# Making the low parts of projection weights on VectorE, and summing the first block's modulation shifts on TensorE

## The chip, the cores and the metric

The kernel runs on one core of a Trainium2 chip. The metric is the device time of one execution in microseconds (us). A core has TensorE (PE in the profile: matmuls, with weight loads as PEld), VectorE (DVE), ScalarE (ACT), GpSimd (POOL) and SyncE (SP), whose queue here issues nearly all DMAs. Each engine works through a queue of its own, in an order that is fixed when the kernel is compiled; semaphores tie the queues together.

## The reference

One layer of a decoder trunk on 512 tokens of width 2048: a conditioned norm, a mixer of two head groups, and a retrieval feed-forward. What matters for the change is the beginning:

```
c_act = jax.nn.silu(c)                                  # one vector of 2048
mod = (c_act @ ada_w[l] + ada_b[l])[:, None, :]         # 2048 x (6*2048)
sh1, sc1, g1, sh2, sc2, g2 = jnp.split(mod, 6, axis=-1)
h = rmsnorm(x, mix_norm_g[l]) * (1.0 + sc1) + sh1
proj = h @ w_in                                         # 2048 x 3920
```

After that come norms of the latents, the up-projections, attention and gated linear attention, the output projection, a second conditioned norm and the feed-forward. The change touches none of these.

## The kernel before

**Products in three parts.** A float32 weight tile is loaded (`wraw`, L267), cast to a rounded high part by ScalarE (`whi`, L115), and the low part is the difference `wlo = wraw - whi` (L117). `split` has an argument that says which engine subtracts: VectorE by default, GpSimd where `load_w` is called with `"gpsimd"`. The activations have parts `hhi` and `hlo` (L303, L304). `mm3` (L107 to L110) then multiplies high by high (L108), high weight by low activation (L109), and low weight by high activation (L110): the low part of the weight is asked for by the third matmul.

**Start.** x arrives in four DMAs of 1 MB. Its squares are summed by VectorE and GpSimd (L163), TensorE sums them over partitions (L167), VectorE makes the reciprocal root (`rstd`, L145 to L151), TensorE spreads it (L156) and ScalarE copies it to `rr` (L206). GpSimd then multiplies the 16 tiles of x by `rr` (L209).

**Modulations.** `mod_acc` sums one section of `c_act @ ada_w` for a range of columns on VectorE: for each of the 16 tiles of 128 rows it loads a piece of `ada_w` (`adaw`, L222, six buffers), multiplies it by the tile's column of `cact` and adds it to `acc` (L226 for the first, L228 for the rest). `mod_col` then sums `acc` over the partitions with one matmul for each 128 columns (L238) and adds the bias (L240); for a scale it also applies the norm's gain (L244). Scales of the first norm go to `A1`, shifts to `B1`.

**First stage.** The 16 tiles of h are worked in five blocks, `KBLOCKS` = 3, 3, 3, 4 and 3 tiles. For each block, all scales and shifts of its columns must be there (`for _ in late`); then ScalarE makes `xT * A1` (L302) and `hhi` (L303), VectorE `hlo` (L304), and 15 tiles of weight columns are multiplied with the block: 9 matmuls each, or 12 in the block of four. From the second block on VectorE adds each result to the earlier ones (L316). While a block is multiplied, `advance(3)` after each weight tile issues the modulations of the next block; these are 32 pieces, 16 for scales and 16 for shifts. Before the first block nothing else is there for TensorE to do, so its 32 pieces stand ahead of all products.

**Second stage.** Eight more weight tiles (`gr`, L428) with all 16 tiles of h, and then the two halves of `w_gv` (L436), 16 pieces each. Beside these, VectorE sums the modulations for later stages, with 128 x 512 pieces, and works on the latents' norms, the rotary tables and the gates. Weights of both stages have five buffers for `wraw` and four each for `whi` and `wlo`; in both, the low parts are made by GpSimd. The up-projections after them have theirs made by VectorE already.

Of the kernel before, what the change touches and what calls it, by code (L numbers as in the profile page):

```python
# [16 lines left out]
OP = mybir.AluOpType  # L17
# [4 lines left out]
P = 128  # L22
T = 512
TB = 4
D = 2048
KD = 16
# [26 lines left out]
KBLOCKS = ((0, 3), (3, 3), (6, 3), (9, 4), (13, 3))  # L53
# [33 lines left out]
def hybrid_layer(ctx, tc, a, out):  # L87
    nc = tc.nc
# [12 lines left out]
    def bank(tag):  # L101
        return cur[tag][0].tile([P, 512], F32, name="b_" + tag, tag=tag)

    mm = nc.tensor.matmul
# [23 lines left out]
    vec = {}  # L128
# [3 lines left out]
    cact = const.tile([P, KD], F32, name="cact")  # L132
    nc.scalar.activation(cact, vec["c_t"], AF.Sigmoid)
    nc.vector.tensor_tensor(out=cact, in0=cact, in1=vec["c_t"], op=OP.mult)
    A1 = const.tile([P, KD], F32, name="A1")
    B1 = const.tile([P, KD], F32, name="B1")
# [52 lines left out]
    hhi, hlo = [[h0[n][:, k, :] if k < NLAT else h1[n][:, k - NLAT, :] for k in range(KD)] for n in range(2)]  # L189
    wp = pools.push("w", RIGHT, bufs=4)  # L190
# [21 lines left out]
    ada_v = a["ada_w"].rearrange("(k p) n -> p k n", p=P)  # L212

    def ada_tile(pool):
        return pool.tile([P, 512], F32, name="adaw", tag="adaw", bufs=NADA)
# [16 lines left out]
    def mod_col(pool, sec, dst, c0, width):  # L232
        for acc in mod_acc(pool, sec, c0, width):
            yield
        b = bank("m")
        n0, nn = c0 // P, width // P
        for n in range(nn):
            mm(b[:, n:n + 1], acc[:, n * P:(n + 1) * P], ones, start=True, stop=True)  # L238
        d = dst[:, n0:n0 + nn]
        nc.vector.tensor_tensor(out=d, in0=b[:, :nn], in1=vec["ada_b_t"][:, sec * KD + n0:sec * KD + n0 + nn],  # L240
                                op=OP.add)
        if sec in (1, 4):
            g = vec["mixg"] if sec == 1 else vec["ffng"]
            nc.vector.scalar_tensor_tensor(out=d, in0=d, scalar=1.0, in1=g[:, n0:n0 + nn], op0=OP.add, op1=OP.mult)  # L244

    def mod_both(pool, c0, width):
        for acc in mod_acc(pool, 5, c0, width):
            yield
        brow = ada_tile(pool)
        nc.sync.dma_start(out=brow[0:1, :], in_=a["ada_b"][:, 5 * D + c0:5 * D + c0 + width])  # L250
        yield
        b = bank("m")
        n0, nn = c0 // P, width // P
        for n in range(nn):
            mm(b[:, n:n + 1], acc[:, n * P:(n + 1) * P], ones, start=True, stop=True)
        nc.vector.tensor_tensor(out=G2[:, n0:n0 + nn], in0=b[:, :nn],
                                in1=vec["ada_b_t"][:, 5 * KD + n0:5 * KD + n0 + nn], op=OP.add)
        b = bank("m")
        mm(b[0:1, :], ones, acc, start=True, stop=False)
        mm(b[0:1, :], ones[0:1, :], brow[0:1, :], start=False, stop=True)  # L260
        nc.scalar.copy(out=acc[0:1, :], in_=b[0:1, :])
        nc.sync.dma_start(out=g2d[:, c0:c0 + width], in_=acc[0:1, :])


    def load_w(pool, src, shape, lo_eng="vector"):
        raw = pool.tile(shape, F32, name="wraw", tag="wraw", bufs=5 if pool is wp else NWRAW)
        nc.sync.dma_start(out=raw, in_=src)  # L267
        return split(pool, raw, shape, "whi", "wlo", lo_eng=lo_eng)
# [6 lines left out]
    def both(*gens):  # L275
        gens = list(gens)
        while gens:
            for g in list(gens):
                try:
                    yield next(g)  # L280
                except StopIteration:
                    gens.remove(g)
# [5 lines left out]
    ada = pools.push("ada", RIGHT)  # L288
# [3 lines left out]
    def first_mods(k0, n):  # L292
        return both(*(mod_col(ada, sec, dst, k0 * P, n * P) for sec, dst in ((1, A1), (0, B1))))

    late = first_mods(*KBLOCKS[0])
    for ib, (k0, n) in enumerate(KBLOCKS):
        for _ in late:
            pass
        late = first_mods(*KBLOCKS[ib + 1]) if ib + 1 < len(KBLOCKS) else iter(())
        for k in range(k0, k0 + n):  # L300
            t = xT[:, k, :]
            nc.scalar.activation(t, t, AF.Copy, scale=A1[:, k:k + 1])  # L302
            nc.scalar.activation(hhi[k], t, AF.Identity, bias=B1[:, k:k + 1])  # L303
            nc.vector.scalar_tensor_tensor(out=hlo[k], in0=t, scalar=B1[:, k:k + 1], in1=hhi[k],  # L304
                                           op0=OP.add, op1=OP.subtract)
        for i, dst in enumerate(dsts):
            src, m = (a["w_misc"], 80) if dst is None else (a["w_feat"][i - (i > 6)], P)
            wh, wl = load_w(wp, src[:, k0:k0 + n, :], [P, n, m], "gpsimd")
            b = bank("pj")
            for j in range(n):  # L310
                mm3(b[:m, :], wh[:, j, :], wl[:, j, :], hhi[k0 + j], hlo[k0 + j], j == 0, j == n - 1)
            for d, p in ((dst, b),) if dst is not None else ((kpe0, b[0:64, :]), (glr, b[64:80, :])):
                if ib == 0:
                    nc.scalar.copy(out=d, in_=p)
                else:
                    nc.vector.tensor_tensor(out=d, in0=p, in1=d, op=OP.add)  # L316
            advance(3)
# [3 lines left out]
    ada = pools.push("ada2", RIGHT)  # L321
# [6 lines left out]
    late = chain(mod_col(ada, sec, d, c * 512, 512) for sec, d in ((2, G1), (4, A2)) for c in range(4))  # L328
# [13 lines left out]
    def proj_tile(pool, src, m, xh, xl, nk, evac, half=4, lo_eng="vector"):  # L342
        b = bank("pj")
        for k0 in range(0, nk, half):
            wh, wl = load_w(pool, src[:, k0:k0 + half, :], [P, half, m], lo_eng)
            for j in range(half):
                k = k0 + j
                mm3(b[:m, :], wh[:, j, :], wl[:, j, :], xh[k], xl[k], k == 0, k == nk - 1)
        evac(b)
# [4 lines left out]
    def gr_evac(i):  # L354
        def f(b):
            nc.scalar.activation(gr[:, i, :], b, AF.Sigmoid)
            nc.vector.tensor_tensor(out=gr[:, i, :], in0=b, in1=gr[:, i, :], op=OP.mult)
        return f
# [66 lines left out]
        nc.scalar.activation(cosT, ang, AF.Sin)  # L425

    for i in range(8):
        proj_tile(wp, a["w_feat"][14 + i], P, hhi, hlo, KD, gr_evac(i), lo_eng="gpsimd")  # L428
        early(i)
        advance(10)  # L430
    ckh, ckl, cqh, cql = [h[i:j] for i, j in ((0, 2), (2, 6)) for h in (hhi, hlo)]
    latents = [ckv[:, i, :] for i in range(2)] + [cq[:, i, :] for i in range(4)]
    for half in range(2):
        bs = [bank("pj") for _ in range(TB)]
        for k in range(KD):
            wh, wl = load_w(wp, a["w_gv"][half, k], [P, 512], "gpsimd")  # L436
            for tb in range(TB):
                tsl = slice(tb * P, (tb + 1) * P)
                mm3(bs[tb], hhi[k][:, tsl], hlo[k][:, tsl], wh, wl, k == 0, k == KD - 1)
            advance(2)  # L440
            if (half, k) == (0, 8):
                gates()
            if (half, k) == (0, 0):
                rotary()
            if half == 1 and k >= NLAT and latents:
                i, src = k - NLAT, latents.pop(0)
                nc.scalar.copy(out=hhi[i], in_=src)
                nc.vector.tensor_tensor(out=hlo[i], in0=src, in1=hhi[i], op=OP.subtract)
        for tb in range(TB):
            nc.scalar.copy(out=gv[:, tb, half * 512:(half + 1) * 512], in_=bs[tb])  # L450
# [7 lines left out]
    kn = qkv.tile([P, MLA_H, T], F32, name="kn")  # L458
# [6 lines left out]
    ada = pools.push("ada3", RIGHT)  # L465
    late = chain(mod_col(ada, 3, B2, c * 512, 512) for c in range(2))
# [42 lines left out]
    for part in range(4):  # L509
        raw = upw.tile([P, 2, 256], F32, name="uraw", tag="uraw4")  # L510
        nc.sync.dma_start(out=raw, in_=a["w_uv"][part])
        wh, wl = split(up, raw, [P, 2, 256], "uhi4", "ulo4")
        for tb in range(TB):
            tsl = slice(tb * P, (tb + 1) * P)
            b = bank("up")
# [141 lines left out]
    for step in SEQ.split():  # L657
        i, n = step[0], [int(v) for v in step[1:].split("-")]
# [35 lines left out]
    late = chain([mod_col(x1p, 3, B2, c * 512, 512) for c in (2, 3)] + [mod_both(x1p, c * 512, 512) for c in range(4)])  # L694
# [10 lines left out]
    for f in range(KD):  # L705
        for g in (0, 1) if f == 0 else (f,) if f > 1 else ():
            first_heads(g)
        b = sums1.pop(f)
        if f % 2 == 0:
            nc.sync.dma_start(out=x1T[:, f:f + 2, :], in_=a["x_t"][:, f:f + 2, :])  # L710
        wh, wl = load_w(ws, a["w_out"][f][:, 0:8, :], [P, 8, P])
# [26 lines left out]
    for t0, m, dst in ((0, P, x1a), (P, NB, x1b)):  # L738
        x1 = x1p.tile([P, D], F32, name="x1", tag="x1", bufs=2)
        for k4 in range(4):  # L740
            b = bank("tr")
# [30 lines left out]
    for h in range(8):  # L772
        tv = rp.tile([P, 2, TB, 16], F32, name="tv", tag="tv")
        ti = rp.tile([P, 2, TB, 16], U32, name="ti", tag="ti")
        for p2 in range(2):
            f = h * 2 + p2
            q = rp.tile([P, T], F32, name="pq", tag="pq")
            b = bank("pj")
            b4 = b.rearrange("p (a b) -> p a b", a=NG)
            for k0 in range(0, KD, 8):  # L780
                wh, wl = load_w(ws, a["w_q"][f][:, k0:k0 + 8, :], [P, 8, P], "gpsimd")
                for j in range(8):
                    k = k0 + j
                    mm3(b4, wh[:, j, :], wl[:, j, :], h2[0][:, :, k, :], h2[1][:, :, k, :], k == 0, k == KD - 1)
            nc.scalar.copy(out=q, in_=b)
            b = bank("sk")
# [10 lines left out]
        for c0, na, nb, a0 in ((0, 4, 16, 0), (64, 12, 4, 4)):  # L797
            shape = [P, TB, na, nb]
            nc.vector.tensor_tensor(out=cd[:, :, c0:c0 + na * nb].rearrange("p t (a b) -> p t a b", b=nb),
                                    in0=tv[:, 0, :, a0:a0 + na].unsqueeze(3).broadcast_to(shape),  # L800
                                    in1=tv[:, 1, :, 0:nb].unsqueeze(2).broadcast_to(shape), op=OP.add)
# [15 lines left out]
        for p2 in range(2):  # L817
# [3 lines left out]
                                    in1=iota16.unsqueeze(1).broadcast_to(shape), op=OP.is_equal)  # L821
            oh4 = oh.rearrange("p (t s) c b -> p t s (c b)", t=TB)
            nc.vector.tensor_tensor(out=oh4, in0=oh4,
                                    in1=tib[:, p2].rearrange("p t c b -> p t (c b)").unsqueeze(2).broadcast_to([P, TB, 8, 32]),
# [73 lines left out]
    for tb in range(1, TB):  # L898
        for n, src in enumerate((flat[tb][0], flat[tb][1], gflat[tb])):
            b = bank("sk")  # L900
# [386 lines left out]
```

## Time and profile before

| | |
|---|---|
| median of 3 runs | 3154.25 us (3148.91 to 3155.24) |
| the profiled execution | 3154.82 us |
| its span, first to last instruction | 3153.1 us |
| PE, DVE, ACT, POOL busy | 96%, 81%, 35%, 26% of the span |
| start until the first product | 0 to 60 us |
| five blocks of the first stage | 60 to 255 us |
| `gr` and `gv` | 255 to 420 us |
| everything after | 420 to 3153 us |

The stage limits are read from TensorE's rows in the trace: the first matmul of a block and of `gr`, the last of `gv`. A stage's table of busy times shows which engine has no room left; the groups of instructions by line give the time of one instruction; the waits say which engine stood for which other.

### The profile page before, as it was taken

The page shows a single profiled execution, that of the slowest core. Times are in us where ns is not written, and L with a number is a line of the kernel's source. Part 1 is how long each engine was busy: PE and PEld are TensorE (multiplying, and loading weights), DVE is VectorE, ACT ScalarE, POOL GpSimd, SP SyncE. Part 2 cuts the span into 40 slices and gives each one's busy share as a digit, 9 for nine tenths or more (in the row PEclk, how much of TensorE's full clock was granted, in tenths as well). Part 3 has the DMA queues.
Part 4 walks back from the last instruction along what each step waited for, and adds up shares of the span by engine and source line. Part 5 has one row for each costly group of instructions (what it writes and reads, how often), then busy time and mean ns, then how long its engine had stood idle before and what let it go on. Part 6 is the DMA issues. An engine that isn't in the chain of part 4 may idle for free.

```text
span 3153.1 us, 46222 instructions
## 1 busy us (share of the span) xinstructions
PE 3037.6 (96%) x17617; PEld 2808.5 (89%) x17617; DVE 2563.7 (81%) x3676; ACT 1111.5 (35%) x1604; POOL 835.0 (26%) x596
## 2 busy tenths in 40 slices
PE   3988999999999999999999999999999999999997
PEld 2777777667777899999999999999999999999997
DVE  8988966677489998688888888888888888888885
ACT  3333344432232355433333333333333333333333
POOL 6445430111233300122222222222222222222210
PEclk9999998999999999999999999999999999999999
DMA  6876943038632257999999999999999999999983
GB/s 219 275 239 197 313 150 101 28 111 287 209 130 85 88 208 262 323 331 350 336 336 335 342 341 337 343 343 333 341 344 335 343 338 340 339 344 338 352 296 121
DMA packets 268527, 850.02 MB, mean 270 GB/s; under 512 B 25768, under 2 KB 99528, under 8 KB 224560
## 3 DMA queue, kind: packets, MB, share of 16 engines
q1 hardware_dynamic: 221712, 511.38, 47.4%
q0 software_dynamic: 46592, 335.68, 28.4%
q8 instruction: 138, 2.26, 0.3%
q14 instruction: 85, 0.70, 0.1%
HBM read 814.74 MB, written 32.19 MB: 269 GB/s over the span
## 4 chain that ended last, share of the span: by engine, by line
PE 84%; DVE 10%; DMA 2%; issue 2%; ACT 1%; SPq 0%; POOL 0%; ACTq 0%; DVEq 0%; POOLq 0%
PE b_p L1080 31%; PE b_p L844 21%; PE b_p L847 10%; PE b_o L703 3%; PE b_pj L109 2%; PE b_pj L110 2%; PE b_pj L108 2%; DVE acc L228 2%; PE b_gg L967 1%; DMA adaw<-in_ada_w 1%; PE b_o L108 1%; PE b_o L109 1%; PE b_o L110 1%; DVE oh L820 1%; PE b_sc L560 1%
## 5 line engine op out<-in xcount | busy, mean ns | idle before, releaser
L115 ACT CAST whi<-wraw 128x1024 fp32r<-128x1024 f32 (+2 forms) x459 | 414.2, 905 | 1036.3 <-PE b_p L844 338.4
L844 PE MATMUL b_p<-h2hi,whi 128*128 128x352 f32 x2048 | 671.4, 328 | 0.0
L844 PE MATMUL b_p<-h2lo,whi 128*128 128x352 f32 x2048 | 666.3, 326 | 0.0
L1080 PE MATMUL b_p<-h2hi,whi 128*128 128x352 f32 x2048 | 655.2, 323 | 0.6 <-DVE xo L1092 0.6
L1080 PE MATMUL b_p<-h2lo,whi 128*128 128x352 f32 x2048 | 653.8, 322 | 0.0
L1074 ACT CAST whi<-wraw 128x1024 fp32r<-128x1024 f32 x256 | 268.7, 1050 | 640.8 <-PE b_p L1080 326.5
L1075 DVE TENSOR_TENSOR wlo<-wraw,whi 128x1024 fp32r<-128x1024 f32 x256 | 312.7, 1223 | 159.6 <-ACT whi L1074 130.0
L117 DVE TENSOR_TENSOR wlo<-wraw,whi 128x1024 fp32r<-128x1024 f32 x282 | 345.0, 1224 | 65.1 <-ACT whi L115 62.0
L844 PEld LDWEIGHTS b_p<-h2lo,whi 128*128 128x128 f32 x2048 | 385.8, 188 | 0.1
L1080 PEld LDWEIGHTS b_p<-h2hi,whi 128*128 128x128 f32 x2048 | 384.4, 188 | 1.4 <-DVE xo L1092 0.9
L844 PEld LDWEIGHTS b_p<-h2hi,whi 128*128 128x128 f32 x2048 | 385.5, 188 | 0.0
L1080 PEld LDWEIGHTS b_p<-h2lo,whi 128*128 128x128 f32 x2048 | 384.9, 188 | 0.0
L228 DVE SCALAR_TENSOR_TENSOR acc<-adaw,cact,acc 128x512 f32<-128x512 f32 (+1 forms) x390 | 356.2, 932 | 29.9 <-DMA adaw<-in_ada_w 24.3
L847 PE MATMUL b_p<-h2hi,wlo 128*128 128x352 f32 x2048 | 377.9, 327 | 0.0
L1080 PE MATMUL b_p<-h2hi,wlo 128*128 128x352 f32 x2048 | 369.8, 322 | 0.0
L117 POOL TENSOR_TENSOR wlo<-wraw,whi 128x512 fp32r<-128x512 f32 (+4 forms) x177 | 277.6, 1576 | 344.5 <-ACT whi L115 333.4
L847 PEld LDWEIGHTS b_p<-h2hi,wlo 128*128 128x128 f32 x2048 | 339.1, 188 | 0.0
L1080 PEld LDWEIGHTS b_p<-h2hi,wlo 128*128 128x128 f32 x2048 | 334.0, 188 | 0.0
L995 POOL DMA_INDIRECT gat<-in_u_rows,eidx x128 | 188.3, 1471 | 510.5 <-ACT whi L1074 201.6
L995 POOL DMA_INDIRECT gat<-in_v_rows,eidx x128 | 185.5, 1449 | 515.6 <-ACT whi L1074 227.8
L1014 DVE SCALAR_TENSOR_TENSOR h2sb<-gat,wt,h2sb 128x2048 f32<-128x2048 f32 x127 | 297.9, 2346 | 26.9 <-DMA gat<-in_v_rows,eidx 26.4
L1001 DVE SCALAR_TENSOR_TENSOR gat<-gat,h2s 128x2048 f32<-128x2048 f32 x128 | 290.8, 2284 | 20.1 <-DMA gat<-in_u_rows,eidx 18.5
(375 smaller groups left out, 4194.1 us busy)
## 6 DMA issues: line engine op xcount, KB each, us to landing
wraw<-in_u_t SPq DMA_DIRECT2D x256, 512.0 KB
wraw<-in_v_t SPq DMA_DIRECT2D x256, 512.0 KB
adaw<-in_ada_w SPq DMA_DIRECT2D x288, 256.0 KB
adaw<-in_ada_w SPq DMA_DIRECT2D x128, 192.0 KB
gd<-stg SPq DMA_DIRECT2D x11, 2048.0 KB
gtile<-gd SPq DMA_DIRECT2D x32, 704.0 KB
wraw<-in_w_out SPq DMA_DIRECT2D x32, 512.0 KB
wraw<-in_w_q SPq DMA_DIRECT2D x32, 512.0 KB
```

The source lines that it names most:

```text
L108: mm(o, wh, xh, start=first, stop=False)
L115: nc.scalar.copy(out=hi, in_=src)
L117: last_lo[0] = e.tensor_tensor(out=lo, in0=src, in1=hi, op=OP.subtract).ins.name
L228: nc.vector.scalar_tensor_tensor(out=acc, in0=w[:, j, :], scalar=cact[:, k:k + 1], in1=acc, op0=OP.mult, op1=OP.add)
L844: mm(b3, uh[:, kk, :], x[:, GA:, k0 + kk, :], start=k0 + kk == 0 and x is h2[0], stop=False)
L847: mm(b3, ul[:, kk, :], h2[0][:, GA:, k0 + kk, :], start=False, stop=k0 + kk == KD - 1)
L995: ins = nc.gpsimd.indirect_dma_start(out=g, out_offset=None, in_=a[table], in_offset=bass.IndirectOffsetOnAxis(ap=idx[:, c:c + 1], axis=0))
L1001: after(nc.vector.scalar_tensor_tensor(out=g, in0=g, scalar=1.0, in1=of(s, h2s, h2sb)[0], op0=OP.mult, op1=OP.mult, accum_out=act0[:, s:s ...
L1014: ins = nc.vector.scalar_tensor_tensor(out=acc, in0=g, scalar=wt0[:, s:s + 1], in1=acc, op0=OP.mult, op1=OP.add)
L1074: pace[0] = nc.scalar.copy(out=vh, in_=vr).ins.name
L1075: pace[1] = nc.vector.tensor_tensor(out=vl, in0=vr, in1=vh, op=OP.subtract).ins.name
L1080: mm(banks[dc][:, :NT], part[:, jj, dc * P:(dc + 1) * P], x, start=first and jj == 0 and part is vh and x is wpair[pair * 2 + jj][0], stop ...
```

## The change

Two things are changed.

1. The calls of `load_w` and `proj_tile` in the first and second stage no longer name GpSimd, so that VectorE makes these low parts: 75 pieces in the five blocks (60 of 128 x 384 or, for one in 15, 128 x 240; 15 of four tiles, 128 x 512 or 128 x 320), 32 of 128 x 512 in `gr` and 32 of 128 x 512 in `gv`.
2. For the first block alone, the shifts (`B1`, section 0) are summed by a new function, `mod_pe`: the same 16 pieces of `ada_w` are loaded into the same six buffers, but each is used as the stationary side of three matmuls with one column of `cact`, which sum in PSUM over all 48. One addition of the bias follows. The scales of the first block and all other modulations stay as they were.

```diff
+    def mod_pe(pool, sec, dst, c0, width):
+        b = bank("m")
+        n, kn = width // P, 512 // width
+        for k0 in range(0, KD, kn):
+            w = ada_tile(pool)[:, :kn * width].rearrange("p (k n) -> p k n", k=kn)
+            nc.sync.dma_start(out=w, in_=ada_v[:, k0:k0 + kn, sec * D + c0:sec * D + c0 + width])
+            for j in range(kn):
+                for i in range(n):
+                    mm(b[:, i:i + 1], w[:, j, i * P:(i + 1) * P], cact[:, k0 + j:k0 + j + 1],
+                       start=k0 + j + i == 0, stop=k0 + j == KD - 1 and i == n - 1)
+            yield
+        i0 = sec * KD + c0 // P
+        nc.vector.tensor_tensor(out=dst[:, c0 // P:c0 // P + n], in0=b[:, :n], in1=vec["ada_b_t"][:, i0:i0 + n], op=OP.add)
+
...
-    late = first_mods(*KBLOCKS[0])
+    late = both(mod_col(ada, 1, A1, 0, KBLOCKS[0][1] * P), mod_pe(ada, 0, B1, 0, KBLOCKS[0][1] * P))
...
-            wh, wl = load_w(wp, src[:, k0:k0 + n, :], [P, n, m], "gpsimd")
+            wh, wl = load_w(wp, src[:, k0:k0 + n, :], [P, n, m])
...
-        proj_tile(wp, a["w_feat"][14 + i], P, hhi, hlo, KD, gr_evac(i), lo_eng="gpsimd")
+        proj_tile(wp, a["w_feat"][14 + i], P, hhi, hlo, KD, gr_evac(i))
...
-            wh, wl = load_w(wp, a["w_gv"][half, k], [P, 512], "gpsimd")
+            wh, wl = load_w(wp, a["w_gv"][half, k], [P, 512])
```

## Rows read from the trace of the kernel before

**Rows 1.** The page's first line: the span.

```profile
span 3153.1 us, 46222 instructions
```

**Rows 2.** Table by stage: PE, PEld, DVE, ACT, POOL busy; PE clock, DMA share, GB/s.

```profile
32.50:60.00 27.50, 2.83 (x13) 2.72 (x13) 26.27 (x23) 2.02 (x4) 24.30 (x16) 1.00 0.51 147
60.00:95.00 35.00, 32.39 (x134) 24.34 (x135) 28.36 (x41) 18.67 (x35) 13.96 (x13) 1.00 0.88 273
95.00:133.00 38.00, 36.40 (x162) 28.59 (x161) 37.58 (x55) 14.12 (x28) 20.30 (x18) 1.00 0.88 276
133.00:177.50 44.50, 38.38 (x157) 30.09 (x155) 39.24 (x53) 12.83 (x23) 18.78 (x16) 0.88 0.77 246
...
255.00:335.00 80.00, 73.57 (x340) 61.20 (x339) 68.12 (x87) 29.19 (x42) 37.54 (x28) 0.96 0.64 213
335.00:420.00 85.00, 85.00 (x372) 67.88 (x371) 77.61 (x76) 34.34 (x57) 42.21 (x28) 0.98 0.80 266
```

**Rows 3.** Instructions by line in 32.6 to 57.2 us: busy, mean ns, idle before.

```profile
L228 DVE SCALAR_TENSOR_TENSOR acc<-adaw,cact,acc 128x384 f32<-128x384 f32 x16 | 24.6, 1607 | 0.4 <-DMA adaw<-in_ada_w 0.4
L209 POOL TENSOR_TENSOR xT<-xT,rr 128x512 f32<-128x512 f32 x16 | 24.3, 1554 | 4.8 <-ACT rr L206 4.8
```

**Rows 4.** DVE in order of time, 20 to 60 us: start, length, instruction.

```profile
29.57 2.73 DVE L228 SCALAR_TENSOR_TENSOR acc<-adaw,cact,acc 128x384 f32<-128x384 f32 x5
32.71 24.55 DVE L228 SCALAR_TENSOR_TENSOR acc<-adaw,cact,acc 128x384 f32<-128x384 f32 x16 [0.41 <-DMA adaw<-in_ada_w]
```

**Rows 5.** PE in order of time, 50 to 62 us.

```profile
55.87 2.95 PE L238 MATMUL b_m<-ones,acc 128*128 128x1 f32 x12 [24.02 <-DVE acc L228]
59.98 1.22 PE L108 MATMUL b_pj<-h0hi,whi 128*128 128x512 f32 x2 [1.16 <-ACT h0hi L303]
```

**Rows 6.** SP's queue in order of time, 24 to 58 us: DMA issues.

```profile
24.62 33.00 SPq L222 DMA_DIRECT2D adaw<-in_ada_w  x28
```

**Rows 7.** Table of two short stretches at the start, columns as in rows 2.

```profile
12.00:16.00 4.00, 0.00 (x0) 0.00 (x0) 3.20 (x4) 3.47 (x7) 3.69 (x3) 1.00 1.01 386
...
28.00:32.00 4.00, 2.05 (x8) 1.78 (x8) 3.97 (x12) 0.12 (x1) 0.00 (x0) 1.00 0.79 237
```

**Rows 8.** DVE and POOL instructions by line in the five blocks, 60 to 255 us.

```profile
L228 DVE SCALAR_TENSOR_TENSOR acc<-adaw,cact,acc 128x384 f32<-128x384 f32 x89 | 67.7, 810 | 5.0 <-DMA adaw<-in_ada_w 4.8
L228 DVE SCALAR_TENSOR_TENSOR acc<-adaw,cact,acc 128x512 f32<-128x512 f32 x55 | 51.2, 953 | 1.1 <-DMA adaw<-in_ada_w 0.7
...
L117 POOL TENSOR_TENSOR wlo<-wraw,whi 128x384 fp32r<-128x384 f32 x54 | 64.9, 1213 | 66.6 <-ACT whi L115 64.8 <-PE b_pj L109 1.8
L117 POOL TENSOR_TENSOR wlo<-wraw,whi 128x512 fp32r<-128x512 f32 x15 | 20.7, 1395 | 28.2 <-ACT whi L115 28.2
```

**Rows 9.** DVE and POOL instructions by line in gr and gv, 255 to 420 us.

```profile
L228 DVE SCALAR_TENSOR_TENSOR acc<-adaw,cact,acc 128x512 f32<-128x512 f32 x89 | 102.3, 1149 | 3.7 <-DMA adaw<-in_ada_w 1.1
...
L117 POOL TENSOR_TENSOR wlo<-wraw,whi 128x512 fp32r<-128x512 f32 x53 | 79.3, 1502 | 79.2 <-ACT whi L115 73.4 <-DMA adaw<-in_ada_w 4.3 <-DMA wraw<-in_w_gv 1.4
```

**Rows 10.** DVE while POOL rests: by line at 450 to 500 us; `adaw`'s users before 58 us (min/median/max).

```profile
L228 DVE SCALAR_TENSOR_TENSOR acc<-adaw,cact,acc 128x512 f32<-128x512 f32 x30 | 22.3, 748 | 1.5 <-DMA adaw<-in_ada_w 1.2
L117 DVE TENSOR_TENSOR ulo<-uraw,uhi 128x512 fp32r<-128x512 f32 x11 | 7.5, 687 | 1.0 <-ACT uhi L115 0.9
...
L228 DVE SCALAR_TENSOR_TENSOR acc<-adaw,cact,acc x30: 605/1562/1618, 20.7 to 55.6; 128x384 f32<-128x384 f32 x30
```

**Rows 11.** Waits of PE and of DVE in the five blocks, 60 to 255 us: total, times, longest.

```profile
PE b_m L238 <- DVE acc L228: 6.0, 2, 5.5
PE b_pj L110 <- POOL wlo L117: 5.2, 9, 1.7
...
DVE acc L226 <- DMA adaw<-in_ada_w: 8.3, 2, 7.7
DVE acc L228 <- DMA adaw<-in_ada_w: 5.5, 7, 2.2
```

**Rows 12.** The longest wait of PE in gr and gv, 255 to 420 us.

```profile
PE b_m L156 <- DVE stat L151: 6.4, 1, 6.4
```

## The prediction

> **What bounds the kernel now.** I read the table by stage first, then the instructions by line and the order of time at the start, last the waits. The span is 3153.1 us [rows 1], and the profiled execution's own time is 3154.82 us, 0.6 us above the median of the runs; the sum below is made against 3154.82. TensorE is the bound nearly everywhere, so a gain can only come from where it stands idle or waits. That is the start above all: from 32.5 to 60 us TensorE is busy for 2.8 of 27.5 us, while VectorE is busy for 26.3 and GpSimd for 24.3 [rows 2]. The reader is to see that in this stretch both do one thing each: VectorE sums 16 pieces of 128 x 384 at 1607 ns, and GpSimd multiplies 16 tiles of x by `rr` at 1554 ns [rows 3]. The same piece takes 605 ns at least [rows 10], and five of them ran in 2.73 us, 0.55 us each, before GpSimd began [rows 4]; once it had, 16 took 24.55 us, 1.53 us each [rows 4]. The two take turns: while GpSimd reads its tile, VectorE's instruction stands still. Only after the last piece come the sums over partitions at 55.87 us, and the first product at 59.98 [rows 5].
>
> In the five blocks VectorE is the second bound. In the second block it is busy for 37.6 of 38.0 us; in the third TensorE's clock falls to 0.88 on average [rows 2], after a wait of 5.5 us for `acc` [rows 11]. In `gv` TensorE is never idle (85.0 of 85.0) and VectorE has 7.4 us to spare [rows 2].
>
> **The start.** `mod_pe` takes 16 of the 32 pieces from VectorE. By 32.3 us VectorE has summed half of the 32, so with scales and shifts in turn 8 of the 16 scales; what is left for it is 8 x 1.53 = 12.3 us, to 44.8. If TensorE frees its buffers sooner, 10 scales are done by then and the rest ends at 41.7. The transfers give a bound of their own. SP issues 28 pieces, some of them the next block's, over 33 us [rows 6], because it waits for buffers. Ten of the first 32 had gone out before; the other 22, 196.6 KB each, are 4.3 MB, which at the 237 GB/s of 28 to 32 us [rows 7] take 18.2 us from 24.6, to 42.8, and one last piece of 1.5 makes it 44.4; at the 386 GB/s that x reaches [rows 7] it would be 37. I take 43 for the end of the scales, between 41.7 and 44.8. On TensorE a one-column matmul costs 2.95 / 12 = 0.25 us [rows 5], so a piece 0.74 us and all 48 some 12 us, on an idle engine and half as long as the 1.5 us in which VectorE does the piece beside it: nothing on the path. Its cost if that cover is gone is the last piece's 0.74. From the first sum over partitions to the first product it is 59.98 - 55.87 = 4.1 us, which stays. So the first product comes at 47.1: **12.9 us earlier** (bounds: 8, if transfers stay at 200 GB/s, and 17, if 12 scales are done by 32.3).
>
> **What GpSimd still owes.** By 47 us GpSimd has done about nine of its 16 multiplications; the other seven now fall into the first block, and each costs VectorE some 1.53 - 0.60 = 0.93 us, 6.5 in all. VectorE was busy there for 28.4 us [rows 2]; with 13 low parts and the relief below it comes to 35.5, against 35 us that the block lasts. I put this at nothing (0 to 5).
>
> **The low parts, on both sides.** One on VectorE takes 687 ns for 128 x 512 [rows 10]; for 128 x 384 I take 0.54 us, less by what a piece of 384 is shorter than one of 512 (605 against 748 ns). Relief comes from GpSimd's silence. In the blocks the pieces of 384 average 810 ns and those of 512 average 953 [rows 8], both 0.205 us over their times alone: 89 x 0.205 + 55 x 0.205 = 29.5 us. Added are 54 x 0.54 + 15 x 0.687, and five smaller ones at 0.45: 41.7 us. VectorE has 12.2 us more to do in 195. In `gr` and `gv`, relief is 89 x (1.149 - 0.748) = 35.7 us [rows 9, 10], added 53 x 0.687 = 36.4: even. So the load barely moves, because a low part on GpSimd already cost VectorE about as much time as making it.
>
> What does this do to TensorE? In the second block VectorE would be busy for 37.6 + 8.0 - 31 x 0.205 = 39.2 us: 1.2 longer. In the third 39.2 + 8.0 - 6.2 = 41.0, and with a microsecond of waiting 42 in place of 44.5: 2.5 shorter, because the sum that TensorE stood for is less late and the clock need not fall. For the other two I take 1.2 shorter together. TensorE's wait for GpSimd's low part, 5.2 us [rows 11], I take as replaced: a low part is made in half of the 1213 to 1502 ns that GpSimd takes [rows 8, 9], but behind one piece on average in VectorE's queue. What is queued behind such a low part is the pieces for the next block and the additions of results (L316). Blocks: **2.5 us less** (bounds: 12.2 more, if VectorE's added time is all on the path; 16 less, if 6.0 and 5.2 us of waits [rows 11] and the slow clock, 0.12 x 44.5 = 5.3, all go). `gr` and `gv`: nothing (4 less to 7 more); the wait of 6.4 us for the latents' statistics [rows 12] stays. Everything after 420 us is as before.
>
> The Trainium skill, in "Perfetto Trace Analysis", section "Optimizing Scalar/DVE Operations", says that where VectorE is saturated, handing some work to ScalarE or even to GpSimd may make sense, and adds that VectorE and GpSimd share a port, so that it might not help between these two. By its first half the low parts should stay on GpSimd, and this change gives the time of the first rival below. By its second half and by rows 3 and 9 the move costs little. The trace bears out the second more.
>
> **The sum.** 3154.8 - 12.9 - 2.5 = 3139.4 us.
>
> **The rivals.**
> - *VectorE takes the gain back.* The 12.2 us of added work in the blocks are all on the path, as VectorE has no room in the second block: 3154.8 - 12.9 + 12.2 = 3154. For: 37.6 of 38.0 us busy. Against: 28.4 of 35 and a wait of 7.7 us in one place, so there is room elsewhere. 0.2.
> - *VectorE's queue stands for transfers, with the low parts behind.* In the blocks VectorE waits 8.3 + 5.5 = 13.8 us for pieces of `ada_w` [rows 11]. Before, the low parts went on beside this on GpSimd; now TensorE's third matmul waits with them. It decides once a wait is longer than the four low parts that can be made ahead, 4 x 35/15 = 9 us of products. With the first rival: 3154 + 13.8 = 3168. For: weights and pieces come through one SP queue, DMA share 0.88. Against: the longest wait is 7.7. 0.13.
> - *The waits in the blocks go as well.* 16 us less there: 3154.8 - 12.9 - 16.5 = 3125. For: the third block's stall comes from pieces that ran at 953 ns. Against: VectorE stays full. 0.12.
> - *The start isn't shortened.* `mod_pe`'s matmuls sit in TensorE's queue, ahead of the sums that `rr` needs, and wait there for pieces; `rr` and GpSimd come late by what is won: 3154.8 - 2.5 = 3152. 0.05.
>
> **How the numbers follow.** The forecast has 0.5, with its own range of 3131 to 3147. A measurement of this kernel can tell 0.2%, 6.3 us, from no change. Faster by more: the forecast and the third rival, 0.62. Within it: the first and the fourth, 0.25 less a little that is slower: 0.24. Slower: 0.14. The range runs from the third rival to beyond the first, 3124 to 3160, and leaves out the second and the ends.
>
> **What would show it.** The first product at 45 to 49 us, with pieces before it at some 1.5 us in VectorE's rows and 48 one-column matmuls on TensorE; pieces of 512 near 0.75 us from 60 to 420 us; low parts at 0.54 and 0.69 us on VectorE; the third block under 43 us. I am wrong if TensorE's waits for low parts on VectorE pass 15 us, or if pieces stay near 1 us with GpSimd silent.

## The result and the profile after

The changed kernel takes 3129.59 us (median of 4 runs, 3128.51 to 3133.64), before 3154.63 beside it: a ratio of 0.993, 95% interval 0.9915 to 0.9944, about 22 us less, or 25 by the two medians. The prediction was 3139.4, with a range of 3124 to 3160. So the direction and the range hold, but most of the gain did not come from where the sum put it, as the marks below show.

The table by stage of the changed kernel, columns and stretches as in [rows 2]. Mind that the changed kernel is 4 us further on in its work at 60 us, and 22 at 420. One stage limit of the profile before needs setting right: 420 us lies in the middle of `gv`, whose first half ends at 412 us and whose second ends at 457. About ten of the 64 low parts of `gr` and `gv` are made after [rows 9] ends. In `gv` the low part of the weight is asked for by the second matmul (L109), not the third.

```profile
32.50:60.00 27.50, 22.58 (x91) 21.02 (x91) 18.54 (x25) 3.90 (x6) 20.98 (x15) 1.00 0.76 229
60.00:95.00 35.00, 35.00 (x158) 28.67 (x157) 29.72 (x60) 20.24 (x39) 0.00 (x0) 1.00 0.90 278
95.00:133.00 38.00, 36.87 (x164) 28.60 (x162) 36.30 (x69) 11.76 (x23) 0.00 (x0) 1.00 0.85 270
133.00:177.50 44.50, 40.05 (x159) 28.05 (x160) 41.18 (x73) 12.89 (x23) 0.00 (x0) 0.96 0.80 252
...
255.00:335.00 80.00, 78.72 (x375) 65.75 (x374) 70.67 (x125) 27.64 (x43) 0.65 (x2) 1.00 0.78 259
335.00:420.00 85.00, 83.94 (x362) 66.68 (x362) 60.26 (x93) 36.25 (x59) 0.00 (x0) 0.98 0.65 212
```

GpSimd is nearly silent after the start (in the stretch left out, 177.5 to 255 us, it is busy for 6.1 us), TensorE is busier in all stages but the last, and from 32.5 to 60 us it is no longer idle: 22.6 of 27.5 us, nearly all of it for the shifts. Here is TensorE in order of time at the start (start, length, instruction); L254 is the matmul of `mod_pe`.

```profile
26.02 2.05 PE L156 MATMUL b_m<-ident,stat 128*128 128x128 f32 x8 [2.51 <-DVE stat L151]
27.86 10.36 PE L254 MATMUL b_m<-cact,adaw 128*128 128x1 f32 x48
38.86 2.72 PE L254 MATMUL b_m<-cact,adaw 128*128 128x1 f32 x12 [0.64 <-DMA adaw<-in_ada_w]
41.80 1.44 PE L254 MATMUL b_m<-cact,adaw 128*128 128x1 f32 x6 [0.22 <-DMA adaw<-in_ada_w]
...
48.40 2.72 PE L254 MATMUL b_m<-cact,adaw 128*128 128x1 f32 x12 [0.39 <-DMA adaw<-in_ada_w]
51.28 1.41 PE L238 MATMUL b_m<-ones,acc 128*128 128x1 f32 x6 [0.16 <-DVE acc L228]
55.59 2.07 PE L108 MATMUL b_pj<-h0hi,whi 128*128 128x512 f32 x4 [2.90 <-ACT h0hi L317]
```

The 48 matmuls stand as 96 instructions: a float32 matmul is two here. They begin only behind L156 and last until 51.1 us. The first product comes at 55.59 us, 4.4 earlier than in [rows 5].

VectorE's instructions by line from 60 to 420 us (busy, mean ns, idle before), to be laid beside [rows 8 to 10]:

```profile
L228 DVE SCALAR_TENSOR_TENSOR acc<-adaw,cact,acc 128x512 f32<-128x512 f32 x150 | 111.8, 756 | 10.4 <-DMA adaw<-in_ada_w 8.7
L117 DVE TENSOR_TENSOR wlo<-wraw,whi 128x512 fp32r<-128x512 f32 x76 | 51.6, 686 | 9.5 <-ACT whi L115 9.2
L228 DVE SCALAR_TENSOR_TENSOR acc<-adaw,cact,acc 128x384 f32<-128x384 f32 x84 | 48.1, 615 | 1.1 <-DMA adaw<-in_ada_w 1.0
L117 DVE TENSOR_TENSOR wlo<-wraw,whi 128x384 fp32r<-128x384 f32 x52 | 28.8, 562 | 2.7 <-ACT whi L115 2.4 <-PE b_pj L110 0.3
```

And TensorE's waits in the same stretch, against [rows 11, 12]:

```profile
PE b_pj L108 <- ACT whi L115: 3.5, 9, 0.8
PE b_pj L110 <- DVE wlo L117: 1.7, 5, 0.7
PE b_m L156 <- DVE stat L151: 1.3, 1, 1.3
PE b_pj L109 <- DVE wlo L117: 1.1, 1, 1.1
```

The pieces have their lone times again (756 and 615 ns), and no wait of TensorE is longer than 1.3 us (2.0 in the second profile of this kernel, at the end of the experiments).

What VectorE has to do as a whole, columns as in [rows 2]: first before, from the first product to the first result of `gr` and from there to the first copy out of `gv`; then the same two pieces of work in the changed kernel.

```profile
60.00:269.80 209.80, 194.36 (x833) 152.23 (x834) 183.60 (x249) 73.42 (x134) 106.28 (x85) 0.98 0.82 260
269.80:412.00 142.20, 135.77 (x607) 110.06 (x606) 126.86 (x146) 53.58 (x82) 61.58 (x45) 0.96 0.70 234
```

```profile
55.60:254.00 198.40, 192.78 (x833) 150.88 (x834) 185.94 (x330) 72.80 (x131) 6.06 (x4) 0.99 0.84 265
254.00:389.90 135.90, 133.55 (x607) 108.31 (x606) 113.11 (x190) 52.67 (x83) 0.65 (x2) 0.99 0.76 253
```

VectorE makes the low parts there, and yet it is busy for only 2.3 us more in the first stretch and for 13.8 us less in the second.

For all that follows, these are the marks of the traces, in us: the start of ScalarE's first `xT * A1` of each block, the first two results of `gr`, the first copy out of `gv`, and the first matmul of the up-projections. "Low parts" and "shifts" are the two parts of the change alone (first two experiments), "blocks" and "gr, gv" the low parts of one stage alone (the next two). "Again" is a second profile of the changed kernel. Each column is one execution, and the two of the changed kernel differ by up to 3.5 us, so a mark that differs by less tells nothing by itself.

| mark | before | changed | again | low parts | shifts | blocks | gr, gv |
|---|---|---|---|---|---|---|---|
| block 1 | 58.0 | 53.6 | 54.1 | 57.4 | 54.7 | 58.7 | 58.1 |
| block 2 | 91.0 | 82.8 | 82.4 | 88.6 | 84.2 | 88.7 | 90.1 |
| block 3 | 125.9 | 116.9 | 120.4 | 124.9 | 121.0 | 124.3 | 124.5 |
| block 4 | 168.4 | 161.0 | 162.9 | 167.2 | 169.5 | 166.6 | 167.0 |
| block 5 | 210.7 | 201.0 | 202.9 | 207.1 | 208.9 | 206.5 | 209.8 |
| gr, first result | 269.8 | 254.0 | 255.9 | 260.1 | 267.2 | 259.7 | 272.6 |
| gr, second result | 290.5 | 268.3 | 270.2 | 274.4 | 286.5 | 281.2 | 287.6 |
| gv, first copy | 412.0 | 389.9 | 391.8 | 397.6 | 407.9 | 404.2 | 412.4 |
| up-projections | 458.3 | 436.9 | 438.8 | 444.6 | 454.3 | 450.6 | 459.4 |

### The profile page after: what moved, and what is told of

It is laid out like the page before. It is cut to its first block, busy times and chain, and to the rows that moved or that the text cites. A ratio compares the mean times of both kernels' runs of the same rounds, so it can differ in the third digit from the quotient of the medians.

```text
span 3126.9 us, 46260 instructions
## 1 busy us (share of the span) xinstructions
PE 3049.3 (98%) x17707; PEld 2823.5 (90%) x17707; DVE 2534.4 (81%) x3799; ACT 1111.1 (36%) x1603; POOL 662.1 (21%) x457
## 4 chain that ended last, share of the span: by engine, by line
PE 88%; DVE 9%; DMA 2%; ACT 1%; issue 1%; SPq 0%; ACTq 0%; DVEq 0%
PE b_p L1094 31%; PE b_p L858 21%; PE b_p L861 10%; PE b_pj L110 4%; PE b_pj L109 3%; PE b_pj L108 3%; PE b_o L717 3%; PE b_gg L981 1%; PE b_o L108 1%; PE b_o L109 1%; PE b_o L110 1%; DVE oh L834 1%; DMA adaw<-in_ada_w 1%; PE b_sc L574 1%; PE b_sc L573 1%
## 5 line engine op out<-in xcount | busy, mean ns | idle before, releaser
L117 DVE TENSOR_TENSOR wlo<-wraw,whi 128x1024 fp32r<-128x1024 f32 (+3 forms) x421 | 431.8, 1028 | 88.0 <-ACT whi L115 83.7
L1089 DVE TENSOR_TENSOR wlo<-wraw,whi 128x1024 fp32r<-128x1024 f32 x256 | 313.4, 1226 | 165.3 <-ACT whi L1088 135.6
L1028 DVE SCALAR_TENSOR_TENSOR h2sb<-gat,wt,h2sb 128x2048 f32<-128x2048 f32 x127 | 298.4, 2349 | 22.1 <-DMA gat<-in_v_rows,eidx 21.4
L1009 POOL DMA_INDIRECT gat<-in_u_rows,eidx x128 | 197.6, 1544 | 501.8 <-ACT whi L1088 196.5
L228 DVE SCALAR_TENSOR_TENSOR acc<-adaw,cact,acc 128x512 f32<-128x512 f32 (+1 forms) x375 | 273.1, 743 | 36.9 <-DMA adaw<-in_ada_w 32.7
L1106 DVE TENSOR_TENSOR xo<-b_p,xo 128x352 f32<-128x352 f32 x236 | 107.3, 518 | 64.1 <-PE b_p L1094 64.0
```

What stands on the lines that cost most here:

```text
L117: last_lo[0] = e.tensor_tensor(out=lo, in0=src, in1=hi, op=OP.subtract).ins.name
L228: nc.vector.scalar_tensor_tensor(out=acc, in0=w[:, j, :], scalar=cact[:, k:k + 1], in1=acc, op0=OP.mult, op1=OP.add)
L1009: ins = nc.gpsimd.indirect_dma_start(out=g, out_offset=None, in_=a[table], in_offset=bass.IndirectOffsetOnAxis(ap=idx[:, c:c + 1], axis=0))
L1028: ins = nc.vector.scalar_tensor_tensor(out=acc, in0=g, scalar=wt0[:, s:s + 1], in1=acc, op0=OP.mult, op1=OP.add)
L1089: pace[1] = nc.vector.tensor_tensor(out=vl, in0=vr, in1=vh, op=OP.subtract).ins.name
```

## The experiments

The theories that the expectations name: A, the gain after the start is GpSimd's silence; B, much of it is a happier order of the queues; C, it is that low parts are ready sooner; D, the wait in `gr` came from the positions' load; E and F, transfers or VectorE's turns with GpSimd set the end of the start. In the run that sums the shifts as a row and in the one that issues the first pieces early, A and B mean something else: A, that TensorE's pieces set the end of the start; B, that transfers do. In the code, `...` stands for lines left out; edits are shown against the changed kernel, or against the kernel before where that is said.

### The two parts alone

Low parts by VectorE, shifts as before:

```
-    late = both(mod_col(ada, 1, A1, 0, KBLOCKS[0][1] * P), mod_pe(ada, 0, B1, 0, KBLOCKS[0][1] * P))
+    late = first_mods(*KBLOCKS[0])
```

> The low parts are made by VectorE as in the changed kernel, but the first block's shifts are summed by VectorE as before. Theory A (the gain after the start comes from GpSimd's silence, and the start's gain from the shifts on TensorE): first product at 58 to 61 us, pieces of 128 x 512 near 0.75 us, and 19 to 22 us less than before in all. Theory B (a good part of the gain is a happier order of the queues, which any edit can give or take): the pieces are as short, but the gain lies anywhere between 5 and 20 us, and PE's waits in gr are again several us.

Measured: ratio 0.9949 (0.9932 to 0.9965), 16 us less. The first product is at 59.4 us as expected, and the wait in `gr` is 1.3 us, as in the changed kernel, where B wanted several. The gain is 3 us short of A's.

Shifts by TensorE, low parts by GpSimd, undoing the other part:

```
-            wh, wl = load_w(wp, src[:, k0:k0 + n, :], [P, n, m])
+            wh, wl = load_w(wp, src[:, k0:k0 + n, :], [P, n, m], "gpsimd")
...
-        proj_tile(wp, a["w_feat"][14 + i], P, hhi, hlo, KD, gr_evac(i))
+        proj_tile(wp, a["w_feat"][14 + i], P, hhi, hlo, KD, gr_evac(i), lo_eng="gpsimd")
...
-            wh, wl = load_w(wp, a["w_gv"][half, k], [P, 512])
+            wh, wl = load_w(wp, a["w_gv"][half, k], [P, 512], "gpsimd")
```

> The first block's shifts are summed by TensorE, and all low parts stay on GpSimd. Both theories: the first product comes at 55 to 56 us, 4 to 5 us earlier than before. Theory A: nothing else moves, 3 to 6 us less than before in all. Theory B: the total can differ from that by 5 us and more either way.

Measured: ratio 0.9985 (0.9975 to 0.9995), 4.7 us less; first scale at 54.7, first product at 56.7 us. The lead is not kept in a straight line: TensorE's waits, 60 to 420 us,

```profile
PE b_m L238 <- DVE acc L228: 9.2, 1, 9.2
PE b_pj L110 <- POOL wlo L117: 6.6, 10, 1.7
PE b_m L156 <- DVE stat L151: 5.2, 1, 5.2
```

show the third block standing for its successor's modulations even longer than before, 9.2 us in place of 5.5 [rows 11]. The block takes 48.5 us from mark to mark in place of 42.5, and at block 4 nothing of the lead is left. It comes back later (4.0 us at the up-projections). The two parts make 20.8 us together, against 22 to 23 for the whole change: within the intervals they add up.

### One stage's low parts alone

Both with the shifts as before; the first keeps the `"gpsimd"` of `gr` and `gv`, the second that of the blocks. They are shown against the kernel before.

```
-            wh, wl = load_w(wp, src[:, k0:k0 + n, :], [P, n, m], "gpsimd")
+            wh, wl = load_w(wp, src[:, k0:k0 + n, :], [P, n, m])
```

> Only the low parts of the five blocks are made by VectorE; those of gr and gv, and the first block's shifts, are as before. Theory A: the blocks end 4 to 6 us earlier, and gr keeps its wait of some 6 us for the statistics; 4 to 7 us less than before. Theory B: the wait in gr is gone here too, with low parts still on GpSimd there, and the gain is 10 us or more.

Measured: ratio 0.9974 (0.9963 to 0.9985), 8 us less, a little above A's 4 to 7. By block 5 it is 4.2 us ahead, by the first result of `gr` 10.1. TensorE keeps its wait for the statistics, against B:

```profile
PE b_m L156 <- DVE stat L151: 7.2, 1, 7.2
```

```
-        proj_tile(wp, a["w_feat"][14 + i], P, hhi, hlo, KD, gr_evac(i), lo_eng="gpsimd")
+        proj_tile(wp, a["w_feat"][14 + i], P, hhi, hlo, KD, gr_evac(i))
...
-            wh, wl = load_w(wp, a["w_gv"][half, k], [P, 512], "gpsimd")
+            wh, wl = load_w(wp, a["w_gv"][half, k], [P, 512])
```

> Only the low parts of gr and gv are made by VectorE; the five blocks and the first block's shifts are as before. Theory A: the blocks end when they did before, and gr and gv take some 12 us less, as in the changed kernel; 10 to 17 us less in all. Theory B: gr and gv gain less than 6 us.

Measured: ratio 0.9993 (0.998 to 1.0005), nothing that can be told. A wanted 10 to 17 us less, with some 12 in `gr` and `gv`, so its forecast failed here. From the first to the second result of `gr` it is 15.0 us in place of 20.7, but from there to the first copy out of `gv` 124.8 in place of 121.5, at a mean granted clock of 0.96 in place of 0.99. That is 2.4 us in all, which is what B's mark allows (less than 6). TensorE had no idle time left in the second part before: 121.5 of 121.5 us busy. Another 3.7 us are lost ahead, from block 5 to the first result of `gr` (62.8 us); the rotary run below takes 63.1 there with the blocks' low parts on GpSimd as here, so this loss need not be due to the edit.

The waits of VectorE and of TensorE from 200 to 300 us, and the instructions about two of them in order of time:

```profile
DVE ang L410 <- DMA posi<-in_positions: 6.6, 1, 6.6
```

```profile
PE b_m L156 <- DVE stat L151: 2.0, 1, 2.0
PE b_pj L110 <- DVE wlo L117: 2.0, 1, 2.0
```

```profile
257.19 0.68 DVE L330 TENSOR_TENSOR gk<-b_pj,gk 128x512 f32<-128x512 f32 x1
257.79 0.68 DVE L117 TENSOR_TENSOR wlo<-wraw,whi 128x512 fp32r<-128x512 f32 x1
...
270.62 0.43 DVE L410 CAST ang<-posi 128x512 f32<-128x512 int32 x1 [6.62 <-DMA posi<-in_positions]
```

```profile
258.52 0.50 PE L110 MATMUL b_pj<-h0hi,wlo 128*128 128x512 f32 x1 [1.97 <-DVE wlo L117]
```

VectorE stands 6.6 us for the positions, but only from 264.0 us on. TensorE's wait of 2.0 us for a low part is over at 258.5; that low part stood behind pieces and additions of results, in a VectorE queue that had not been idle since 253.6. So the second rival, a low part held up behind a transfer, is not seen here either. The two stages alone make 10 us, together 16; the intervals don't rule out that they add up.

### GpSimd made to read again

```
...
+        if pool is wp:
+            spare = pool.tile(shape, F32R, name="spare", tag="spare", bufs=1)
+            nc.gpsimd.tensor_tensor(out=spare, in0=raw, in1=hi, op=OP.subtract)
```

> The changed kernel, but GpSimd makes each low part of the two stages a second time into a tile that nobody reads; VectorE's low parts are used as in the changed kernel. Theory A (GpSimd's reading holds up VectorE, and silence is what the change gains after the start): pieces of 128 x 512 go back to 1.0 to 1.2 us, VectorE has some 70 us more to do in 60 to 420 us than in the changed kernel and becomes the bound; the time is 3155 to 3200 us, slower than before. Theory C (the gain comes from low parts that are ready sooner, and the share of the port does not matter): no more than 5 us above the changed kernel.

Measured: 3198.87 us, ratio 1.0149 (1.0132 to 1.0166): 48 us slower than before, 69 above the changed kernel. VectorE by line, TensorE's waits, and the table, all for 60 to 420 us:

```profile
L228 DVE SCALAR_TENSOR_TENSOR acc<-adaw,cact,acc 128x512 f32<-128x512 f32 x122 | 122.6, 1018 | 2.7 <-DMA adaw<-in_ada_w 1.4
...
L117 DVE TENSOR_TENSOR wlo<-wraw,whi 128x512 fp32r<-128x512 f32 x54 | 44.0, 818 | 0.8 <-ACT whi L115 0.8
```

```profile
PE b_pj L110 <- DVE wlo L117: 29.7, 32, 4.3
PE b_m L156 <- DVE stat L151: 9.5, 2, 8.3
```

```profile
60.00:420.00 360.00, 312.19 (x1320) 238.72 (x1319) 344.83 (x475) 104.05 (x181) 154.79 (x120) 0.97 0.70 218
```

Nobody reads what GpSimd makes, yet VectorE's pieces go from 756 to 1018 ns and its low parts from 686 to 818, it is busy for 344.8 of 360 us, and TensorE waits 29.7 us for low parts and up to 8.3 for the statistics in `gr`. C falls, A stands. The Trainium skill, in "SBUF — State Buffer", section "Who interferes with whom", says that a VectorE instruction with two inputs from SBUF contends with a GpSimd instruction that reads SBUF, because the second input comes through a read interface that both share. These rows agree with it: both of VectorE's instructions here have two inputs, and they are longer by 262 and 132 ns. (The spare product also keeps `wraw` and `whi` longer, so not all of the 69 us need be the reading.)

### The wait in gr

The rotary tables, which need the positions, are called ahead of `gr` (against the kernel before):

```
+    rotary()
     for i in range(8):
...
-            if (half, k) == (0, 0):
-                rotary()
```

> The kernel before, with the call of the rotary tables moved ahead of gr, so that the positions are loaded earlier and VectorE's queue does not stand 4.9 us for them in front of the latents' statistics. Theory D (that wait for the positions is why PE waits 6.4 us for the statistics in gr, and the change only moved it out of the way): PE's wait falls below 2 us, and the time is 5 to 8 us less than before. Theory A (the statistics are late because VectorE's queue is long beside GpSimd): the wait stays above 4 us, 0 to 3 us less.

Measured: ratio 1.0002 (0.9991 to 1.0012). TensorE's wait for the statistics is 4.2 us in two, the longest 3.8, where A wanted more than 4 and D less than 2:

```profile
PE b_m L156 <- DVE stat L151: 4.2, 2, 3.8
```

From the first to the second result of `gr` it is 18.4 us in place of 20.7. D explains a part of the wait at most, and no gain in the whole. The wait is 7.2 us in the run of the blocks alone, where GpSimd makes `gr`'s low parts, 2.0 where VectorE does, and 8.3 where VectorE makes them and GpSimd reads beside it: it hangs on GpSimd's reading in `gr`.

### What sets the end of the start

The shifts summed as a row, with the sides of the matmul exchanged:

```
...
-                    mm(b[:, i:i + 1], w[:, j, i * P:(i + 1) * P], cact[:, k0 + j:k0 + j + 1],
-                       start=k0 + j + i == 0, stop=k0 + j == KD - 1 and i == n - 1)
+            mm(b[0:1, :width], cact[:, k:k + 1], w, start=k == 0, stop=k == KD - 1)
...
+        nc.scalar.copy(out=row[0:1, :width], in_=b[0:1, :width])
+        b = bank("m")
+        for i in range(n):
+            mm(b[:, i:i + 1], row[0:1, i * P:(i + 1) * P], ones[0:1, :], start=True, stop=True)
```

> The changed kernel with the first block's shifts summed the other way round: a column of cact is the stationary side and the piece of ada_w the moving one, one matmul for a piece in place of three; the row of 384 that results is copied and turned into columns by three small matmuls. Theory A (in the changed kernel TensorE's 1.41 us for each of 16 pieces, begun at 27.9 us, set the end of the start): a piece costs 0.6 to 0.8 us, TensorE waits for transfers instead, VectorE's 16 scales at up to 1.5 us set the end near 43 to 46 us, and the first product comes at 48 to 51 us, 5 to 7 us earlier than in the changed kernel, which is 25 to 30 us less than before. Theory B (the transfers of the 32 pieces set the end): first product at 54 to 56 us as in the changed kernel.

Measured: 3132.34 us, ratio 0.9935 (0.9919 to 0.9952), as the changed kernel. TensorE in order of time:

```profile
37.08 0.81 PE L252 MATMUL b_m<-adaw,cact 128*1 128x384 f32 x2 [0.51 <-DMA adaw<-in_ada_w]
...
55.36 2.07 PE L108 MATMUL b_pj<-h0hi,whi 128*128 128x512 f32 x4 [2.32 <-ACT h0hi L319]
```

A piece alone costs 0.81 us in place of 1.44, and the first product is where it was: A, that TensorE's pieces alone set the end, fell. Something else is due at the same time. Two variants of this kernel ask what. First, the first block's weights put behind the pieces on SP:

```
...
+        ins = nc.sync.dma_start(out=raw, in_=src)
+        if pool is wp and last_ada[0]:
+            tc.add_manual_dep(ins.ins, last_ada[0], mybir.DependencyInfo(mybir.DependencyClass.NoSync, mybir.DependencyReason.DATA), reason="pace")
```

> The kernel with the shifts summed as a row, and the first block's weights issued on SP only after all 32 pieces of the first modulations. Theory E (eight weight loads, 1.7 MB, that now go out ahead of the pieces set the end of the start there): first product at 47 to 51 us, but the first block begins without weights and takes back most of it; 0 to 5 us from the changed kernel. Theory F (VectorE's turns with GpSimd set the end): first product at 54 us or later.

Measured: 3133.96 us, ratio 0.9943 (0.9927 to 0.996). First product at 53.9 us, between E and F and 1.5 earlier than in the row run. But the stretch was not cleared. SP now issues four loads of up-projection weights there, 768 KB, of which the row run issues one at 30.8 us and the others from 55.7 us on:

```profile
21.65 0.43 SPq L496 DMA_DIRECT2D uraw<-in_w_ukn  x1
...
22.78 0.44 SPq L496 DMA_DIRECT2D uraw<-in_w_uqn  x1
...
24.90 0.43 SPq L496 DMA_DIRECT2D uraw<-in_w_uqp  x1
25.38 0.43 SPq L496 DMA_DIRECT2D uraw<-in_w_ukn  x1
```

So the 1.5 us are the price of a part of the loads only. Second, GpSimd's later products of x held back:

```
-    for k in range(KD):
+    for k in range(3):
         nc.gpsimd.tensor_tensor(out=xT[:, k, :], in0=xT[:, k, :], in1=rr, op=OP.mult)
...
+        for k in range(3, KD) if ib == 0 else ():
+            ins = nc.gpsimd.tensor_tensor(out=xT[:, k, :], in0=xT[:, k, :], in1=rr, op=OP.mult)
+            tc.add_manual_dep(ins.ins, last_mod[0], mybir.DependencyInfo(mybir.DependencyClass.Sync, mybir.DependencyReason.DATA), reason="pace")
```

> The kernel with the shifts summed as a row, and 13 of GpSimd's 16 products of x with rr held back until the first modulations are done. Theory F: VectorE's pieces fall to 0.6 us after the third product, first product at 46 to 51 us; the first block is then up to 12 us longer, as GpSimd reads beside it; within 6 us of the changed kernel either way. Theory E: pieces are as short, but VectorE waits for transfers, and the first product stays at 53 us or later.

Measured: 3140.66 us, ratio 0.9972 (0.9961 to 0.9984), 12 us above the changed kernel. VectorE in order of time:

```profile
41.45 0.62 DVE L228 SCALAR_TENSOR_TENSOR acc<-adaw,cact,acc 128x384 f32<-128x384 f32 x1 [1.25 <-DMA adaw<-in_ada_w]
42.49 0.62 DVE L228 SCALAR_TENSOR_TENSOR acc<-adaw,cact,acc 128x384 f32<-128x384 f32 x1 [0.42 <-DMA adaw<-in_ada_w]
```

The pieces are at 0.62 us, and VectorE then waits for transfers; the first product still comes at 53.65 us. So F falls (without VectorE's turns the first product is 1.7 us earlier than in the row run), and of E the main part holds: behind TensorE's and VectorE's work the arrival of the pieces is due within 2 us of the same time. What paces the arrival (the loads ahead of them, the six buffers, the transfers themselves) is open. The first block then takes 39.5 us from mark to mark in place of 29.2, with GpSimd's 13 products in it: TensorE waits 4.8 us for `hlo` and 3.1 for low parts there.

Last, TensorE's first pieces issued ahead of the statistics, in the changed kernel:

```
+    for _ in range(8):
+        next(late)
     ss = bank("m")
     col_sums(ss, 0, totals[0])
...
```

> The changed kernel with the first four pieces of scales and of shifts issued ahead of the statistics of x, so that TensorE can begin its pieces before the sums that rr needs. Theory A: three of the 16 pieces lie before 26 us, TensorE ends some 4 us earlier, first product at 51 to 53 us; as TensorE's pieces stand ahead of those sums, rr comes up to 1 us later. Theory B: no earlier than 54 us.

Measured: 3132.33 us, ratio 0.9939 (0.9922 to 0.9955), as the changed kernel. The first scale comes at 49.6 us, 4 earlier, and the first product at 51.6, but TensorE then waits 3.5 us for `hlo`, which stands in VectorE's queue while GpSimd still multiplies (its products begin at 32.25 in place of 30.30 us). Block 2 begins at 83.8 us, 1 later than in the changed kernel. Its first product is the earliest of all runs, and two things differ: TensorE's pieces begin sooner, and no load of weights goes out ahead of the pieces. The first is at

```profile
42.23 0.42 SPq L271 DMA_DIRECT2D wraw<-in_w_feat  x1
```

So this run fits E as well as TensorE's earlier beginning, and doesn't tell them apart.

### The changed kernel once more

> The changed kernel itself, beside the next two on one chip. 20 to 25 us less than before; TensorE's half-speed time between 500 and 650 us may differ from the first profile by 10 us and more, with the same order of work.

Measured: 3128.11 us, ratio 0.9927 (0.9911 to 0.9944), beside 3148.57 for the kernel before. Its marks are the column "again" above.

## Why the prediction was right, and where it was not

In the whole it was right: 15.4 us less forecast, some 22 to 25 measured, inside the range and between the forecast and the third rival. By its steps it was right by two misses of opposite sign; that the total came out is in good part luck.

| step | forecast | measured, first profile | second profile |
|---|---|---|---|
| start, to the first product | -12.9 | -4.4 | -3.9 |
| blocks, to the first result of `gr` | -2.5 | -11.3 | -10.0 |
| from there to the first copy out of `gv` | 0 | -6.4 | -6.4 |
| everything behind that copy | 0 | -4.0 | -4.8 |

**The start: the term that was mis-sized is TensorE's.** I divided [rows 5]'s 2.95 us by 12 and took 0.25 us for a matmul. The row counts instructions, and the line (L238) does three matmuls for scales and three for shifts, six in all: 0.49 us each. The 48 of `mod_pe` keep TensorE busy for 21.4 us, a piece 1.34, not half of VectorE's 1.5 but nearly as long. Nor did I place them: their queue begins at 27.9 us, behind L156, so they end at 51.1, with 1.8 us of waiting for transfers. And the bound that I worked out from transfers, 44.4 us, was too early as well: in the changed kernel eight loads of weights go out ahead of the pieces between 17 and 29 us, where there were two. That comes with both parts of the change together: the low-parts run has two such loads, the shifts run five. By 32 us VectorE had summed six of the 16 scales, not eight, and the last ended at 51.1, not 43. The row experiment shows that mending the first miss alone would have gained nothing.

**GpSimd's debt** in the first block was nearly nothing, because the block began at 55.6 and not at 47; the experiment that holds 13 products back until then has a first block that is 10 us longer.

**The low parts: the lone times are right, the load on VectorE and its use by TensorE were not.** Lone times were forecast at 0.54 and 0.69 us for a low part (measured 0.562 and 0.686) and 0.605 and 0.748 for a piece (0.615 and 0.756). But the load came out as 2.3 us more in the blocks, where 12.2 were forecast, and 13.8 less in `gr` and the first half of `gv`, where it was to stay even. The relief was counted for the pieces alone, and other instructions got shorter too: those that make `hlo` of the later tiles from 1090 to 745 ns, the scans for the gates from 1740 to 1210. VectorE's instructions of 0.68 us also begin 0.60 us apart when they run back to back, as in the lines of the `gr`, `gv` run. And I let the waits that GpSimd causes stand: 5.2 us for low parts "replaced", 6.4 us for the statistics kept. Both nearly went: for low parts of VectorE TensorE waits 1.7 and 1.1 us (3.6 and 1.1 in the second profile), for the statistics 1.3.

The runs show which edit does it. From block 5 to the first result of `gr` it is 53.0 to 53.2 us wherever VectorE makes the blocks' low parts (changed, again, low parts, blocks) and 58.2 to 63.1 where GpSimd does (before, shifts, gr and gv, rotary). Between the first two results of `gr` it is 14.3 to 15.0 us where VectorE makes `gr`'s, and 18.4 to 21.6 where GpSimd does. Behind the second result nothing is gained up to the first copy out of `gv` (121.5 us before, 121.5 and 121.6 after). A part of the gain is the granted clock, which comes back with the waits. By the clock columns here and in [rows 2], an estimate for the stretches shown: 0.12 x 44.5 + 0.04 x 80 + 0.02 x 85 = 10 us lost to it before, 0.04 x 44.5 + 0.02 x 85 = 3.5 in the changed kernel.

The third block was forecast at 42 us, 2.5 less. From mark to mark it takes 42.5 before and 44.1 and 42.5 in the two profiles of the changed kernel, so the forecast gain is not seen there. The first block took 29.2 in place of 33.0; what of it is owed to which edit was not taken apart.

**The rivals.** The first, VectorE takes the gain back, fell with VectorE at 36.3 of 38 us in the second block and 29.7 of 35 in the first. The second was not seen: TensorE's waits for low parts stay under 5 us in all in both profiles, and in the `gr`, `gv` run the one low part that TensorE waited 2.0 us for was not behind a transfer. The third, the waits in the blocks go as well, is what happened, in about two thirds of its size. The fourth, shifts behind the statistics on TensorE, has its order reversed: the shifts stand behind the statistics and are late themselves.

## What to carry to other kernels

An elementwise pass given to GpSimd was not free for a busy VectorE here: measure the same VectorE instruction with GpSimd silent and with it reading, and count what each GpSimd instruction takes from it, before calling GpSimd's time hidden. When a matmul's price is taken from a row, count the matmuls that the line does, since a row may count two instructions for each float32 matmul. When a sum over pieces is split between engines, find the next thing due (here transfers, VectorE and TensorE lie within some 2 us) before pricing the gain.

## What the runs showed that was not expected

After the up-projections the granted clock drops to 1.2 GHz for a time that differs from run to run, with TensorE at work throughout. Before the change, and then the changed kernel at the same place in the work (columns as in [rows 2]):

```profile
525.00:545.00 20.00, 20.00 (x49) 10.47 (x49) 9.08 (x30) 5.59 (x14) 0.00 (x0) 0.50 0.00 0
```

```profile
503.00:513.00 10.00, 10.00 (x26) 5.02 (x25) 5.33 (x15) 2.50 (x7) 0.00 (x0) 0.54 0.00 0
513.00:523.00 10.00, 10.00 (x56) 6.69 (x57) 7.54 (x24) 3.59 (x10) 0.00 (x0) 1.00 0.01 2
```

From 480 to 680 us the trace's clock record has 24 us at half speed before, 14 in both profiles of the changed kernel, 31 in the low-parts run and 7 in the rotary run, though nothing was edited in that stage. The low-parts run's profile took 3146.5 us at a mean clock of 0.988, its other three 3135.7 to 3139.9 at 0.991 to 0.992. From the first matmul of the up-projections to the end the profiles take 2687 us (rotary run) to 2700 (low-parts run); 2695 before, 2690 and 2689 in the changed kernel. So the 4 to 5 us that the last line of the table above gives come out twice, but are not shown to belong to the change.
